# A hybrid decoder layer on one core: low-rank columns as 256 and 448, recurrence and attention values of four heads per 512-column product, the output gate ahead of the queries in every second pair

## The chip, the cores and the metric

The kernel runs on one core of a Trainium2 chip. The metric is the device time in microseconds (us) of one execution; lower is better. The kernel before takes 638.74 us (median of three runs, 638.66 to 638.91).

Engines are named as in the profile: PE is the matrix engine (PEld its loads of the stationary operand), DVE the vector engine, ACT the scalar engine, POOL the GpSimd engine, SP the queue that issues most transfers. "Product" below means one matmul instruction: a stationary block of 128x128 and a moving block of 128 rows and N columns.

## What is computed

One decoder layer on x of 512 tokens by 1024 channels, float32:

```python
h = rms_norm(x, norm_g)
hq, hf, hi, hz, cq, ckv, kr, mz, glog = split(h @ w_in)   # 1024 x4, 384, 256, 64, 1024, 2048 columns
y_a = hgrn2_branch(hq, hf, hi, hz)     # 8 heads of 128: forget gate, query, value, output gate
y_b = mla_branch(cq, ckv, kr, mz)      # 8 heads, causal attention from low-rank columns
gates = sigmoid(glog + b_gate)
merged = gates[0] * (y_a @ w_proj_a) + gates[1] * (y_b @ w_proj_b)
out = rms_norm(x + merged @ w_out, final_norm_g)
```

The HGRN2 branch is a gated linear recurrence in chunks of 32 tokens; the attention branch first widens 384 low-rank query columns and 256 low-rank key/value columns per head (weights `w_uq`, `w_ukv`).

## The kernel before

Every float32 matrix is split in two parts, a rounded high part (`hi`) and the rest (`lo`), and each product of the reference is three products on PE (`mm3`: hi by hi, hi by lo, lo by hi; lines 90 to 92). `load_w` brings 512 KB of weights to `w_raw` (3 buffers) by a transfer on SP, ACT writes `w_hi` (4 buffers, line 111) and DVE `w_lo` (4 buffers, line 112). I call one such load a piece.

There are two kinds of projections of h. `proj_ch` gives channels by tokens: a 128x128 block of weights stands still and 512 tokens of `hT` move, 48 products of 512 columns for 256 channels, from two pieces. `proj_tok` gives tokens by channels: a block of `hT` stands still and the weights move, so the moving block is as wide as the piece of columns, 256 or 192 here. Both write to `mm_ps`, a pool of 3 banks of the accumulator memory; other products write to `ax_ps`, 5 banks.

The stages, in order of the program:

1. Start (lines 195 to 327, engine orders written out by hand): the row `norm_g` is spread over 128 partitions by a product with ones (`ng`, line 274); four token blocks are normalized (`xn`, line 237), transposed (line 245) and split to `hT`; the first 256 low-rank columns are multiplied on the way (line 256). Products of zeros (`idle_mm`, line 221) keep PE running.
2. The other low-rank columns, 256 and then 192 wide, through `proj_tok`.
3. Four pairs of HGRN2 heads (`hg_pair`): forget gates (`proj_ch`), values of two heads (`proj_tok`, 256 columns), queries, output gate, then chunk scores (lines 488 to 496), outputs (507, 509) and the gate's product. `hg_forget` on DVE is long: a scan (432) and a reciprocal (433) among others.
4. Eight attention heads; `mla_values` makes the values of two heads in one call (256 columns), every second head.
5. Two merge projections, the output projection, and the last norm token block by token block.

Outside stage 1 a scheduler that simulates the engines sets the order of instructions on each engine, so the order of the program's text is not the order of the queues.

Of the kernel before, what the change touches and what calls it, by code (L numbers as in the profile page):

```python
# [9 lines left out]
F32 = mybir.dt.float32  # L10
# [8 lines left out]
P = 128  # L19
# [19 lines left out]
def hybrid_layer(ctx: ExitStack, tc: tile.TileContext, a):  # L39
# [92 lines left out]

    def proj_tok(mat, c0, w, lhs, halves=None):

        halves = halves or load_cols(mat, c0, w)
        ps = []
        for t2 in range(NT // 2):
            b = mm_tile()
            for t in range(2):
                tt = 2 * t2 + t  # L140
                for kk in range(KD):
                    mm3(b[:, t * 256 : t * 256 + w], lhs, halves[kk // 4],
                        (slice(None), kk, slice(tt * P, tt * P + P)), (slice(None), kk % 4),
                        kk == 0, kk == KD - 1)
            ps.append(b)
        return ps

# [24 lines left out]
    zero = st.tile([P, 512], BF16, "zero")  # L172
    ones = st.tile([P, P], F32, "ones")
    ones_r = st.tile([P, P], F32R, "ones_r")
    warm = st.tile([P, 1], F32, "warm")
    ng_row = st.tile([1, D], F32, "ng_row")
    ng_z = st.tile([P, D], F32, "ng_z")
    ng_r = [st.tile([P, D], F32R, f"ng_r{i}") for i in range(2)]
    x_sb = [st.tile([P, D], F32, "x", bufs=NT) for _ in range(NT)]
# [15 lines left out]
    load_x(0, 2)  # L195
    nc.scalar.dma_start(ng_row[:], a["norm_g"])
    nc.scalar.dma_start(ident[:], a["c_ident"])
# [53 lines left out]
    def c_product(t, kh, kind, ks=range(4)):  # L251
# [3 lines left out]
        for k in ks:  # L255
            nc.tensor.matmul(ps, hT[l][:, 4 * kh + k, t * P : t * P + P], c_hl[kh][r][:, k * 256 : k * 256 + 256],  # L256
                             start=kh == 0 and kind == 0 and k == 0, stop=kh == 1 and kind == FIN and k == 3)

    FIN = 1
    with tc.manual_schedule(engines={mybir.EngineType.PE, mybir.EngineType.Activation, mybir.EngineType.DVE}):  # L260
        nc.vector.memset(zero[:], 0.0)
        nc.vector.memset(ones[:], 1.0)
        nc.vector.tensor_copy(ones_r[:], ones[:])
        nc.vector.memset(ng_z[:], 0.0)
        for i in range(2):
            nc.vector.tensor_copy(ng_r[i][:], ng_z[:])
        nc.scalar.activation(warm[:], eps, AF.Sqrt)
        idle_mm(6)

        nc.vector.tensor_copy(ng_r[0][0:1], ng_row[:])  # L270
        nc.vector.tensor_tensor(ng_r[1][0:1], ng_row[:], ng_r[0][0:1].bitcast(F32), op=ALU.subtract)
        for x in range(2):
            for n in range(2):
                nc.tensor.matmul(ng[n][:], ones_r[:], ng_r[x][:, half[n]], start=x == 0, stop=x == 1)
            idle_mm(3)

# [35 lines left out]
        for t in range(1, NT):  # L312
            if t + 2 < NT:
                squares(t + 2)
            for kh in range(2):
                lo[kh]()
            if t + 1 < NT:
                scaled(t + 1)
            else:
                c_second = load_cols(w_in, COL_C + 256)  # L320
# [42 lines left out]

    for c0, w in ((0, 256), (256, 256), (512, 192)):
        for t2, ps in enumerate(proj_tok(w_in, COL_C + c0, w, hT, c_second if c0 == 256 else None) if c0 else c_ps):
            nc.scalar.copy(c_sb[:, 2 * t2 : 2 * t2 + 2, c0 : c0 + w],
                           ps[:].rearrange("p (t c) -> p t c", t=2)[:, :, :w])
    css = cw.tile([P, 2, NT], F32, "css")
# [97 lines left out]
    def hg_states(h, k128, ft, v_sb):  # L466
# [7 lines left out]
        for i in range(NT - 1):  # L474
            sl = slice(i * P, i * P + P)
            nc.tensor.matmul(sps[:, sl], kt_[:, sl], v_sb[:, i, (h % 2) * P : (h % 2) * P + P], start=True, stop=True)  # L476
        nc.vector.tensor_copy(st_[:, 0:P], sps[:, 0:P])
# [24 lines left out]
    def hg_out(h, asb, st_, q128, v_sb):  # L502

        ops = ax_tile()
        for i in range(NT):
            sl = slice(i * P, i * P + P)
            nc.tensor.matmul(ops[:, sl], asb[:, sl], v_sb[:, i, (h % 2) * P : (h % 2) * P + P], start=True, stop=i == 0)  # L507
            if i:
                nc.tensor.matmul(ops[:, sl], q128[:, sl], st_[:, i * P - P : i * P], start=False, stop=True)  # L509
# [16 lines left out]
    def silu2(z, pz):  # L526

        nc.scalar.activation(z, pz, AF.Tanh, scale=0.5)
        nc.vector.scalar_tensor_tensor(z, z, 1.0, pz, op0=ALU.add, op1=ALU.mult)

    def hg_pair(pair, before_gate=None, before_out=None):
# [5 lines left out]
        for t2 in range(2):  # L537
            nc.scalar.copy(v_sb[:, 2 * t2 : 2 * t2 + 2].rearrange("p t c -> p (t c)"), vps[t2][:])
# [6 lines left out]
        zz = [z_tile() for _ in hs]  # L545
        for i in range(2):
            silu2(zz[i][:], pz[i][:])
        aa = [hg_scores(h, kk[i][2], kk[i][3], kk[i][4], qq[i][0], qq[i][1]) for i, h in enumerate(hs)]
# [38 lines left out]

    def mla_values(pair):
# [3 lines left out]
        for t2 in range(2):  # L592
            ps = mm_tile()
            for t in range(2):
                tt = 2 * t2 + t
                for k in range(2):
                    mm3(ps[:, t * 256 : t * 256 + 256], cT, wv, (slice(None), 3 + k, slice(tt * P, tt * P + P)),
                        (slice(None), k), k == 0, k == 1)
            split(*[x[:, 2 * t2 : 2 * t2 + 2].rearrange("p t c -> p (t c)") for x in v], ps[:])
        return v  # L600
# [56 lines left out]
    def mla_out(h, pts, v, z):  # L657
        ops = mm_tile()
        for j in range(NT):
            mm3(ops[:, j * P :], v, pts[j], (slice(None), j, slice((h % 2) * P, (h % 2) * P + P)), (slice(None),),  # L660
                j == 0, j == NT - 1)
        nc.vector.tensor_tensor(yb[:, h], ops[:], z[:], op=ALU.mult)
# [28 lines left out]
    for h in range(H):  # L691
# [7 lines left out]
        if h + 1 < H:  # L699
            nope = mla_nope(h + 1, pools[(h + 1) % 2])  # L700
        if h % 2 == 0:
            v = mla_values(h // 2)
        if late:
            mla_out(*late)
        hook = lambda: mla_transpose(pn)
        if h + 1 == H:
# [56 lines left out]

    def out_mm(k, t, n, w):
        mm3(acc[t][n][:], m, w, (slice(None), k, slice(t * P, t * P + P)),
            (slice(None), 0, slice(n * 512, n * 512 + 512)), k == 0, k == KD - 1)

    for k in range(4):
        w = load_wo(k)
        for t in range(NT):  # L770
            for n in range(2):
                out_mm(k, t, n, w)
    ws = [load_wo(k) for k in range(4, KD)]
# [3 lines left out]
    for t in range(NT):  # L777
        ss = op.tile([P, 2], F32, "ss", bufs=2)
        xs = [xr[t][:, n * 512 : n * 512 + 512] for n in range(2)]
        rg = [op.tile([P, 512], F32, f"rg{n}", bufs=2) for n in range(2)]  # L780
        for n in range(2):
            for k in range(4, KD):
                out_mm(k, t, n, ws[k - 4])
            nc.vector.scalar_tensor_tensor(xs[n], acc[t][n][:], 0.5, xs[n], op0=ALU.mult, op1=ALU.add)
            sq = op.tile([P, 512], F32, "sq", bufs=2)
            nc.scalar.activation(sq[:], xs[n], AF.Square, accum_out=ss[:, n : n + 1])
            nc.vector.tensor_tensor(rg[n][:], xs[n], fg[:, n * 512 : n * 512 + 512], op=ALU.mult)
            if n == 0:
                nc.gpsimd.tensor_scalar(ss[:, 0:1], ss[:, 0:1], 1.0 / D, EPS, op0=ALU.mult, op1=ALU.add)
        nc.gpsimd.tensor_scalar(ss[:, 0:1], ss[:, 1:2], 1.0 / D, ss[:, 0:1], op0=ALU.mult, op1=ALU.add)  # L790
        nc.gpsimd.tensor_tensor(ss[:, 0:1], ss[:, 0:1], neg_half[:, 0:1], op=ALU.pow)
        o = a["out"][0, t * P : t * P + P, :]
        nc.scalar.activation(rg[0][:], rg[0][:], AF.Copy, scale=ss[:, 0:1])
        nc.scalar.dma_start(o[:, 0:512], rg[0][:])
        nc.vector.tensor_scalar(rg[1][:], rg[1][:], ss[:, 0:1], None, op0=ALU.mult)
        nc.sync.dma_start(o[:, 512:1024], rg[1][:])
    wop.close()
# [42 lines left out]
```

## Time and profile before

| | |
|---|---|
| median of three runs | 638.74 us |
| profiled execution, its own time | 638.65 us |
| its span, first to last instruction | 636.9 us |
| PE busy | 627.3 us (99%), 3539 products |
| DVE, ACT, POOL busy | 353.9, 239.4, 115.4 us |
| moved by transfers | 59.80 MB, mean 94 GB/s |
| granted PE clock | 0.997 |

The profile is of one execution. A product's duration in it includes its pipeline, and products overlap: what a product costs in a stream is the distance from its start to the next one's start, which is read from the timeline. Busy shares alone say little about a stage; the rows of single instructions are used below.

### The profile page before, as it was taken

To read this page: it belongs to the slowest core of one execution; us is meant where nothing else is said; L and a number is where in the kernel's file an instruction comes from. 1 tells how busy PE (TensorE), PEld (TensorE's weight loads), DVE (VectorE), ACT (ScalarE), POOL (GpSimd) and SP (SyncE) were. 2 spreads that over 40 slices of the span, in tenths; PEclk is the share of its full clock that TensorE was granted. 3 is DMA by queue.
4 is the path that set the end of the run, shared out by engine and by line. 5 is a ranking of instruction groups with operands and counts; after the bars stand their busy time and mean duration, and the time that the engine had idled before them with its cause. 6 is when DMAs were issued, how large, how long until landed. Compare 5 with 4: busy or idle time off the path is not lost.

```text
span 636.9 us, 9069 instructions
## 1 busy us (share of the span) xinstructions
PE 627.3 (99%) x3539; PEld 540.1 (85%) x3539; DVE 353.9 (56%) x550; ACT 239.4 (38%) x453; POOL 115.4 (18%) x213
## 2 busy tenths in 40 slices
PE   8999999999999999999999999999999999999995
PEld 5998988988898898888888988888888888888884
DVE  7716973785486387547485857845322342434244
ACT  5535333232322323345454555534222232323223
POOL 2105310320331132221223132000000010111011
PEclk9999999999999999999999999999999999999998
DMA  7443242233124013312324142133333323324403
GB/s 248 137 125 100 67 138 62 67 99 100 34 68 131 13 55 102 92 45 66 104 56 115 51 138 78 37 100 99 100 98 94 98 75 102 102 95 158 173 11 121
DMA packets 61945, 59.80 MB, mean 94 GB/s; under 512 B 5799, under 2 KB 57293, under 8 KB 61902
## 3 DMA queue, kind: packets, MB, share of 16 engines
q1 hardware_dynamic: 59628, 55.47, 29.3%
q10 hardware_dynamic: 2130, 3.22, 1.6%
q8 instruction: 28, 0.46, 0.3%
q0 software_dynamic: 144, 0.52, 0.3%
q14 instruction: 15, 0.12, 0.1%
HBM read 55.01 MB, written 2.10 MB: 90 GB/s over the span
## 4 chain that ended last, share of the span: by engine, by line
PE 97%; DVE 1%; ACT 0%; issue 0%; POOLq 0%; POOL 0%
PE mm_ps L90 26%; PE mm_ps L92 26%; PE mm_ps L91 26%; PE ax_ps L91 2%; PE ax_ps L90 2%; PE ax_ps L92 2%; PE ax_ps L631 2%; PE mm_ps L256 1%; PE ax_ps L652 1%; PE ax_ps L488 1%; PE ax_ps L507 1%; PE ax_ps L509 1%; PE ax_ps L476 1%; PE ax_ps L496 1%; PE ax_ps L493 1%; PE ax_ps L523 1%
## 5 line engine op out<-in xcount | busy, mean ns | idle before, releaser
L112 DVE TENSOR_TENSOR w_lo<-w_raw,w_hi 128x1024 fp32r<-128x1024 f32 (+3 forms) x92 | 109.0, 1186 | 114.5 <-ACT w_hi L111 110.0
L90 PE MATMUL mm_ps<-hT,w_hi 128*128 128x512 f32 x384 | 151.3, 394 | 0.0
L111 ACT CAST w_hi<-w_raw 128x1024 fp32r<-128x1024 f32 (+3 forms) x92 | 89.8, 977 | 163.0 <-PE mm_ps L91 110.6
L92 PE MATMUL mm_ps<-hT,w_lo 128*128 128x512 f32 x384 | 150.2, 392 | 0.0
L91 PE MATMUL mm_ps<-hT,w_hi 128*128 128x512 f32 x384 | 149.8, 390 | 0.0
L92 PEld LDWEIGHTS mm_ps<-hT,w_lo 128*128 128x128 f32 x384 | 72.1, 188 | 14.8
L91 PEld LDWEIGHTS mm_ps<-hT,w_hi 128*128 128x128 f32 x384 | 72.2, 188 | 14.3
L90 PEld LDWEIGHTS mm_ps<-hT,w_hi 128*128 128x128 f32 x384 | 72.2, 188 | 14.1
L92 PE MATMUL mm_ps<-w_hi,hT 128*128 128x256 f32 (+1 forms) x192 | 54.1, 282 | 0.0
L91 PE MATMUL mm_ps<-w_lo,hT 128*128 128x256 f32 (+1 forms) x192 | 54.0, 282 | 0.0
L90 PE MATMUL mm_ps<-w_hi,hT 128*128 128x256 f32 (+1 forms) x192 | 54.0, 282 | 0.0
L742 POOL TENSOR_TENSOR ma<-ma,z 128x512 f32<-128x512 f32 x8 | 11.8, 1478 | 161.3 <-DVE z L741 161.3
L639 POOL TENSOR_SCALAR p<-p,sm 128x128 f32<-128x128 f32 (+3 forms) x32 | 20.6, 647 | 105.1 <-DVE sm L638 53.5
L91 PEld LDWEIGHTS mm_ps<-w_lo,hT 128*128 128x128 f32 x192 | 36.5, 190 | 0.2
L90 PEld LDWEIGHTS mm_ps<-w_hi,hT 128*128 128x128 f32 x192 | 36.4, 190 | 0.2
L92 PEld LDWEIGHTS mm_ps<-w_hi,hT 128*128 128x128 f32 x192 | 36.5, 190 | 0.0
L433 DVE RECIPROCAL tf<-pr 128x512 f32<-128x512 f32 x8 | 26.8, 3349 | 0.2
L637 ACT ACTIVATE p<-ax_ps,sm 128x128 f32<-128x128 f32 (+3 forms) x32 | 16.8, 528 | 22.0 <-DVE sm L636 21.5
L90 PE MATMUL mm_ps<-ya,w_hi 128*128 128x512 f32 x64 | 25.0, 390 | 0.0
L91 PE MATMUL mm_ps<-ya,w_hi 128*128 128x512 f32 x64 | 24.9, 389 | 0.0
L92 PE MATMUL mm_ps<-ya,w_lo 128*128 128x512 f32 x64 | 24.9, 389 | 0.0
L92 PE MATMUL mm_ps<-yb,w_lo 128*128 128x512 f32 x64 | 24.9, 389 | 0.0
(224 smaller groups left out, 1142.7 us busy)
## 6 DMA issues: line engine op xcount, KB each, us to landing
w_raw<-w_in SPq DMA_DIRECT2D x60, 512.0 KB, 3.8
w_raw<-w_proj_a SPq DMA_DIRECT2D x8, 512.0 KB, 3.5
w_raw<-w_proj_b SPq DMA_DIRECT2D x8, 512.0 KB, 3.4
wo_raw<-w_out SPq DMA_DIRECT2D x8, 512.0 KB, 3.2
w_raw<-w_ukv SPq DMA_DIRECT2D x16, 128.0 KB, 2.5
xr<-x SPq DMA_DIRECT2D x4, 512.0 KB, 6.5
x<-x SPq DMA_DIRECT2D x3, 512.0 KB, 8.7
w_raw<-w_uq SPq DMA_DIRECT2D x8, 192.0 KB, 2.6
```

Of the source, the lines that this page charges most:

```text
L90: nc.tensor.matmul(ps, lh[lsl], rh[rsl], start=start, stop=False)
L91: nc.tensor.matmul(ps, lh[lsl], rl[rsl], start=False, stop=False)
L92: nc.tensor.matmul(ps, ll[lsl], rh[rsl], start=False, stop=stop)
L111: nc.scalar.copy(hi[:, :o], raw[:, :o])
L112: (lo_eng or nc.vector).tensor_tensor(lo[:, :o], raw[:, :o], hi[:, :o].bitcast(F32), op=ALU.subtract)
L256: nc.tensor.matmul(ps, hT[l][:, 4 * kh + k, t * P : t * P + P], c_hl[kh][r][:, k * 256 : k * 256 + 256], start=kh == 0 and kind == 0 and k ...
L433: nc.vector.reciprocal(rp[:], pr[:])
L476: nc.tensor.matmul(sps[:, sl], kt_[:, sl], v_sb[:, i, (h % 2) * P : (h % 2) * P + P], start=True, stop=True)
L631: nc.tensor.matmul(sps[:, :n], qh[:, bl], kpe[x][:, :n], start=False, stop=x == 1)
L637: nc.scalar.activation(p[:, :n], sps[:, :n], AF.Exp, scale=SCALE, bias=sm[:, 1:2], accum_out=sm[:, 2:3])
L639: nc.gpsimd.tensor_scalar(p[:, :n], p[:, :n], sm[:, 3:4], 0.5, op0=ALU.mult, op1=ALU.mult)
L742: nc.gpsimd.tensor_tensor(ma[:, j], ma[:, j], g[:], op=ALU.add)
```

## The change

What moves, in the order of the program:

- The start spreads `norm_g` by products over 64 instead of 128 rows: its two halves stand in rows 0 and 32, and `pick` chooses one. The preparation on DVE works on 64x512 instead of 128x1024; zeros and ones come from POOL. One idle product instead of three stands between the two pairs of products, four instead of three after them.
- The remaining 448 low-rank columns are one product per token block and k, from four pieces of 2 k by 448 columns instead of four pieces of 4 k by 256 or 192.
- `proj_tok` takes 512 columns, values of four heads, two token blocks at a time, from four pieces of 2 k by 512. It is called in pairs 0 and 2 only, and its result stays for the next pair.
- In pairs 1 and 3 the output gate's projection stands in the place of the values, between forget gates and queries.
- `mla_values` makes values of four heads in one call, at heads 0 and 4, with one buffer instead of two, and is called behind the output product of the head before.
- In the last norm both halves of a token block share a buffer, and for the last block ACT scales 384 columns and DVE 640 instead of 512 each.

```diff
-    def proj_tok(mat, c0, w, lhs, halves=None):
-        halves = halves or load_cols(mat, c0, w)
-        ps = []
+    def proj_tok(mat, c0, lhs, done):
+        v = mat[:, c0 : c0 + 512].rearrange("(k p) c -> p k c", p=P)
+        w = []
         for t2 in range(NT // 2):
...
+            ps = [mm_tile() for _ in range(2)]
+            for k in range(KD):
+                if t2 == 0 and k % 2 == 0:
+                    w.append(load_w(v[:, k : k + 2, :]))
+                for t in range(2):
+                    tt = 2 * t2 + t
+                    mm3(ps[t][:], lhs, w[k // 2], (slice(None), k, slice(tt * P, tt * P + P)), (slice(None), k % 2),
+                        k == 0, k == KD - 1)
             for t in range(2):
...
+                done(2 * t2 + t, ps[t])
...
+        for i in range(2):
+            nc.vector.tensor_copy(ng_r[i][:], zf[:])
...
         for x in range(2):
             for n in range(2):
-                nc.tensor.matmul(ng[n][:], ones_r[:], ng_r[x][:, half[n]], start=x == 0, stop=x == 1)
-            idle_mm(3)
+                nc.tensor.matmul(ng[n][:], pick_r[:, n], ng_r[x][:], start=x == 0, stop=x == 1)
+            idle_mm(1 + 3 * x)
...
-    for c0, w in ((0, 256), (256, 256), (512, 192)):
...
+    c_second += [load_c2(j) for j in range(2, 4)]
+    for t in range(NT):
+        ps = mm_tile()
+        for k in range(KD):
+            mm3(ps[:, 0:448], hT, c_second[k // 2], (slice(None), k, slice(t * P, t * P + P)), (slice(None), k % 2),
+                k == 0, k == KD - 1)
+        nc.scalar.copy(c_sb[:, t, 256:704], ps[:, 0:448])
...
-        vps = proj_tok(w_in, COL_I + cc, 256, hT)
-        v_sb = hw.tile([P, NT, 256], F32, "v", 2)
...
+        if pair % 2 == 0:
+            for t in range(NT):
+                v_sb[t] = hw.tile([P, 512], F32, f"v{t}")
+            proj_tok(w_in, COL_I + cc, hT, lambda t, ps: nc.scalar.copy(v_sb[t][:], ps[:]))
+        else:
+            zz = gate()
         pq = proj_ch(w_in, COL_Q + cc, hT)
...
-        pz = proj_ch(w_in, COL_ZA + cc, hT)
...
+        if pair % 2 == 0:
+            zz = gate()
...
-        wv = load_w(w_ukv[:, :, 2 * pair : 2 * pair + 2, 128:256])
-        v = [mw.tile([P, NT, 256], F32R, f"v{i}", 2) for i in range(2)]
+        wv = load_w(w_ukv[:, :, h0 : h0 + 4, 128:256])
+        v = [mw.tile([P, NT, 512], F32R, f"v{i}") for i in range(2)]
...
+        c = 384 if last else 512
+        nc.scalar.activation(rg[:, :c], rg[:, :c], AF.Copy, scale=ss[:, 0:1])
+        nc.scalar.dma_start(o[:, :c], rg[:, :c])
+        nc.vector.tensor_scalar(rg[:, c:], rg[:, c:], ss[:, 0:1], None, op0=ALU.mult)
+        nc.sync.dma_start(o[:, c:], rg[:, c:])
```

How the queues change shows at three places. The first is PE at the start of the low-rank columns (stage 2). In a row, `mm_ps` with its number is the accumulator tile of a token block, `w_hi` and `w_lo` with their numbers are a piece, and a number at the end is the moving width. Before:

```order
L334 MATMUL ax_ps_398<-ident_103,rows_98 128x38
L90 MATMUL mm_ps_426<-w_hi_359,hT0_119 128x256
L91 MATMUL mm_ps_426<-w_lo_360,hT0_119 128x256
L92 MATMUL mm_ps_426<-w_hi_359,hT1_120 128x256
L90 MATMUL mm_ps_426<-w_hi_359,hT0_119 128x256
```

Now:

```order
L347 MATMUL ax_ps_401<-ident_103,rows_98 128x38
L90 MATMUL mm_ps_441<-w_hi_362,hT0_123 128x448
L91 MATMUL mm_ps_441<-w_lo_363,hT0_123 128x448
L92 MATMUL mm_ps_441<-w_hi_362,hT1_124 128x448
L90 MATMUL mm_ps_441<-w_hi_362,hT0_123 128x448
L91 MATMUL mm_ps_441<-w_lo_363,hT0_123 128x448
L92 MATMUL mm_ps_441<-w_hi_362,hT1_124 128x448
L90 MATMUL mm_ps_441<-w_hi_368,hT0_123 128x448
L90 MATMUL mm_ps_467<-w_hi_362,hT0_123 128x448
L91 MATMUL mm_ps_467<-w_lo_363,hT0_123 128x448
```

A piece now holds two k instead of four; the scheduler turns to the second token block (467) before the first is done, and the last piece (436, 437) is first read after 42 products.

The second place is PE at the scores of pair 1 (`qi`, `ki`, `ko` and the 64-wide `q64`, `k64` are operands of the scores; `v` and `kt` belong to the states). Before:

```order
L476 MATMUL ax_ps_1568<-v_1465,kt_1563 128x128 x3
L488 MATMUL ax_ps_1644<-qi_1533,ki_1318 128x128 x4
```

Now:

```order
L92 MATMUL mm_ps_1548<-hT0_123,w_lo_1557 128x512
L494 MATMUL ax_ps_1449<-v0_763,kt_1444 128x128
L494 MATMUL ax_ps_1449<-v1_764,kt_1444 128x128
L494 MATMUL ax_ps_1449<-v2_765,kt_1444 128x128
L506 MATMUL ax_ps_1457<-qi_1414,ki_1244 128x128 x4
L511 MATMUL ax_ps_1457<-qi_1414,ko_1245 32x32 x8
L514 MATMUL ax_ps_1457<-q64_1416,k64_1247 64x64 x4
L506 MATMUL ax_ps_1475<-qi_1423,ki_1273 128x128 x4
L511 MATMUL ax_ps_1475<-qi_1423,ko_1274 32x32 x8
L514 MATMUL ax_ps_1475<-q64_1425,k64_1276 64x64 x4
L90 MATMUL mm_ps_1671<-w_hi_1674,hT0_123 128x512
```

Before, the 48 products ahead of these states and scores were those of the output gate. Now (tile 1548, piece 1557) they are the forget products of pair 2, which the scheduler has moved ahead of the scores of pair 1; the values of pair 2 (tile 1671) follow the scores.

The third place is DVE around the same scores; `asb` is the masked score block that the outputs need, `f`, `pr`, `tf`, `ki` belong to the forget gates of the next pair. Before:

```order
L480 SCALAR_TENSOR_TENSOR st_1569<-st_1569,ft_1345,ax_ps_1568 128x128
L529 SCALAR_TENSOR_TENSOR z_1639<-z_1639,mm_ps_1577 128x512
L497 COPY_PREDICATED asb0_730<-mask_le_405,ax_ps_1644 128x512
L480 SCALAR_TENSOR_TENSOR st_1569<-st_1569,ft_1345,ax_ps_1568 128x128
L497 COPY_PREDICATED asb1_734<-mask_le_405,ax_ps_1662 128x512
```

Now:

```order
L446 TENSOR_SCALAR f_1610<-tf_1609,c1_421,c2_423 128x512
L450 SCALAR_TENSOR_TENSOR pr_1616<-f_1610,fr_633 128x512
L451 RECIPROCAL tf_1617<-pr_1616 128x512
L495 COPY st_1450<-ax_ps_1449 128x128
L112 TENSOR_TENSOR w_lo_1729<-w_raw_1727,w_hi_1728 128x1024
L515 COPY_PREDICATED asb0_637<-mask_le_408,ax_ps_1457 128x512
L466 TENSOR_TENSOR ki_1630<-k_1611,tf_1617 128x512
L498 SCALAR_TENSOR_TENSOR st_1450<-st_1450,ft_1271,ax_ps_1449 128x128
L515 COPY_PREDICATED asb1_641<-mask_le_408,ax_ps_1475 128x512
```

A scan, a reciprocal and the last piece of the values now stand ahead of `asb0` on DVE.

More of the change, by code (lines that the diff above doesn't have):

```diff
@@ L319, in hybrid_layer @@
             else:
-                c_second = load_cols(w_in, COL_C + 256)
+                c_second = [load_c2(j) for j in range(2)]
             for kind in (0, 1, 2):
@@ L534, in hg_pair, with gate @@
         kk = [hg_forget(h, pf[i]) for i, h in enumerate(hs)]
[L535 to L538 removed]
+        def gate():
+            pz = proj_ch(w_in, COL_ZA + cc, hT)
+            zz = [z_tile() for _ in hs]
+            for i in range(2):
+                silu2(zz[i][:], pz[i][:])
+            return zz
+        if pair % 2 == 0:
[4 more added lines that the diff above has]
+            zz = gate()
         pq = proj_ch(w_in, COL_Q + cc, hT)
```

108 lines of the change are left out of this document (48 added, 60 removed).

## Prediction

> **What bounds the kernel now.** I read the shares first, then the chain that ended last, then what PE waited for.
>
> ```profile
> PE 627.3 (99%) x3539; PEld 540.1 (85%) x3539; DVE 353.9 (56%) x550; ACT 239.4 (38%) x453; POOL 115.4 (18%) x213
> PE 97%; DVE 1%; ACT 0%; issue 0%; POOLq 0%; POOL 0%
> PE ax_ps L221 <- DVE zero L261: 1.2, 1, 1.2
> PE ax_ps L274 <- DVE ng_r L270: 0.7, 1, 0.7
> PE ax_ps L245 <- DVE xn L237: 0.4, 1, 0.4
> ...
> ```
>
> The second row is the chain's share by engine, the others are PE's waits (total, times, longest). The longest three are 2.3 us together and all belong to the start, as do the two left out. Behind the start PE runs one stream of products without a break that the profile names, so a saving must come from what a product costs in this stream, from the start, or from the 7 us behind the last product. A product costs the distance between starts. The timeline of PE gives it for each width:
>
> ```profile
> 27.30 0.39 PE L90 MATMUL mm_ps<-w_hi,hT 128*128 128x256 f32 x1
> 38.91 0.25 PE L90 MATMUL mm_ps<-w_hi,hT 128*128 128x192 f32 x1
> 49.61 0.41 PE L90 MATMUL mm_ps<-hT,w_hi 128*128 128x512 f32 x1
> 50.78 0.40 PE L92 MATMUL mm_ps<-hT,w_lo 128*128 128x512 f32 x1
> ...
> 117.97 0.28 PE L90 MATMUL mm_ps<-w_hi,hT 128*128 128x256 f32 x1
> 129.48 0.40 PE L90 MATMUL mm_ps<-hT,w_hi 128*128 128x512 f32 x1
> ...
> 290.09 0.36 PE L90 MATMUL mm_ps<-w_hi,cT 128*128 128x256 f32 x1
> 291.61 0.40 PE L90 MATMUL ax_ps<-kn,qn 128*128 128x128 f32 x2
> ...
> 308.95 0.33 PE L90 MATMUL mm_ps<-pt,v 128*128 128x384 f32 x1
> 309.48 0.28 PE L90 MATMUL mm_ps<-pt,v 128*128 128x256 f32 x1
> ...
> 616.23 0.39 PE L90 MATMUL ax_ps<-wo,m 128*128 128x512 f32 x1
> 629.61 0.39 PE L92 MATMUL ax_ps<-wo,m 128*128 128x512 f32 x1
> ```
>
> Width 256: 96 products from 27.30 to 38.91, 0.121 us each, and 96 from 117.97 to 129.48, 0.120. Width 192: 96 from 38.91 to 49.61, 0.1115. Width 384: three from 308.95 to 309.48, 0.177. Width 512: 616.23 and 629.61 are the first and the last of 60 products, 13.38/59 = 0.2268; right behind the low-rank columns, 49.61 to 50.78, five take 0.234 each. So two products of 256 cost 0.240 and one of 512 costs 0.227 to 0.234: 6 to 13 ns less per pair, and 192 costs almost as much as 256.
>
> **Low-rank columns.** Removed: 22.31 us (27.30 to 49.61). Added: 4 token blocks x 8 k x 3 = 96 products of 448 columns, a width the trace lacks. Between its neighbours 384 and 512: (0.177 + 0.227)/2 = 0.202; on the line from 256 to 512: 0.120 + 0.75 x 0.107 = 0.200. At 0.201 they take 19.3 us. Gain 3.0; ends 2.8 (0.203) and 3.2 (0.199). The copies of the result to `c_sb` and the four pieces are as many elements as before, on ACT and DVE. The last piece must wait for a slot in the 3 raw buffers, as the last one did before, but its first use stands 42 products (8.4 us) into the stage, against a cast and a subtraction of 2.3 us (rows below).
>
> **Values of the recurrence.** Removed: 4 x 11.51 = 46.04 us. Added: 2 x 96 products of 512. At 0.2268 they take 43.55, at 0.234 they take 44.9; gain between 1.1 and 2.5. Most products of that stage follow each other in a stream, so I take 0.2285, near the lower price: 43.9, gain 2.2.
>
> **Values of attention.** Removed: 12 products from 290.09 to 291.61, 1.52 us, and 84 more at 0.120: 11.6. Added: 48 of 512, 10.9 to 11.2. Gain 0.7 (0.4 to 0.7), and I keep 0.6.
>
> **The start.** Here the row of `norm_g` is late:
>
> ```profile
> 2.63 1.29 DVE L266 CAST ng_r<-ng_z 128x1024 fp32r<-128x1024 f32 x2
> 3.84 0.68 DVE L270 CAST ng_r<-ng_row 1x1024 fp32r<-1x1024 f32 x1
> 4.55 1.21 DVE L271 TENSOR_TENSOR ng_r<-ng_row,ng_r 1x1024 fp32r<-1x1024 f32 x1
> 5.47 0.19 ACT L280 ACTIVATION_READ_ACCUMULATOR sq<-x 128x1 f32 x1
> 5.69 0.13 DVE L281 TENSOR_SCALAR rsq<-rs 128x1 f32<-128x1 f32 x1
> 6.54 1.41 PE L274 MATMUL ax_ps<-ng_r,ones_r 128*128 128x512 f32 x2
> 7.56 1.41 DVE L237 SCALAR_TENSOR_TENSOR xn<-x,rs,ax_ps 128x512 f32<-128x512 f32 x2 [0.59 <-PE ax_ps L274]
> 10.61 0.36 SPq L208 DMA_DIRECT2D maskf<-c_masks  x1
> SPq L208 <- DMA w_raw<-w_in: 1.1, 1, 1.1
> 11.32 1.14 ACT L224 CAST w_hi<-w_raw 128x512 fp32r<-128x512 f32 x2
> ```
>
> `xn` waited 0.59 us for the spread row. Half the width makes DVE's two casts of 0.65 each half as long, so the real row's conversion starts near 3.0 instead of 3.84 (POOL's fill of zeros and ones must land first) and ends about 0.8 us earlier; the statistics chain behind it, which began at 5.69 only because DVE was busy, then begins with the second sum (5.66). Both together allow `xn` near 6.8: 0.75 us earlier. One idle product between the pairs instead of three lets the second pair follow. A bound from above is the transfer of the second piece, landed at 10.6 (SP's wait), for ACT's cast at 11.32: 0.7. From below: nothing gained, if POOL's fill or the row's transfer comes late. I take 0.6. Later stages follow it one to one, since their waits are on the same chain.
>
> **Behind the last product.**
>
> ```profile
> 632.58 0.72 ACT L793 ACTIVATE rg<-rg,ss 128x512 f32<-128x512 f32 x1 [1.10 <-POOL ss L791]
> 632.58 0.49 DVE L795 TENSOR_SCALAR rg<-rg,ss 128x512 f32<-128x512 f32 x1 [1.13 <-POOL ss L791]
> 633.09 0.33 SPq L796 DMA_DIRECT2D out<-rg  x1
> 633.33 0.34 ACTq L794 DMA_DIRECT2D out<-rg  x1
> ```
>
> ACT's transfer leaves last. With 384 columns ACT needs about 0.58, DVE with 640 about 0.6, so both leave near 633.2: gain 0.1 (0 to 0.2).
>
> **What is moved, and its cover.** These groups (count, busy, mean ns) price the work beside PE, and two rows of PE's timeline begin and end the scores of a pair:
>
> ```profile
> L112 DVE TENSOR_TENSOR w_lo<-w_raw,w_hi 128x1024 fp32r<-128x1024 f32 x74 | 93.3, 1263 | 106.4 <-ACT w_hi L111 106.2
> L433 DVE RECIPROCAL tf<-pr 128x512 f32<-128x512 f32 x8 | 26.8, 3349 | 0.2
> L432 DVE TENSOR_TENSOR_SCAN pr<-f,fr 128x512 f32<-128x512 f32 x8 | 9.8, 1222 | 5.7 <-POOL fr L429 5.7
> L497 DVE COPY_PREDICATED asb<-mask_le,ax_ps 128x512 f32<-128x512 uint8 x8 | 5.8, 731 | 5.1 <-PE ax_ps L496 5.1
> L111 ACT CAST w_hi<-w_raw 128x1024 fp32r<-128x1024 f32 x74 | 77.8, 1052 | 148.9 <-PE mm_ps L91 100.0 <-issue 34.6 <-PE mm_ps L92 13.8
> L538 ACT COPY v<-mm_ps 128x512 f32<-128x512 f32 x8 | 4.7, 584 | 2.1 <-PE mm_ps L92 2.1
> ...
> 153.38 1.06 PE L488 MATMUL ax_ps<-qi,ki 128*128 128x128 f32 x8
> 157.72 0.50 PE L90 MATMUL mm_ps<-hT,w_hi 128*128 128x512 f32 x1
> ```
>
> The values of four heads read a new piece every 12 products, 2.7 us, in their first half, and hold all four slots. The last piece waits for the forget product's last slot, then 1.05 us on ACT and 1.26 on DVE, possibly behind a reciprocal of 3.35: 5.7 us, needed after 36 products, 8.2 us. Covered, with 2.5 us to spare. In the second half the fourth token block needs the bank of the first, whose copy takes 0.58, one group of three products (0.68) plus 0.68 after it ended: 0.8 us to spare. Pieces of the following product get a slot 2.7 us into the second half and need 2.3 of the 8.2 left.
>
> In pair 1 the gate no longer stands between queries and scores; the queue of PE shows pair 2's 48 forget products there, 10.9 us, and the query chain is an ACT instruction and a few of DVE and POOL of the sizes above. But on DVE the forget chain of pair 2 now stands ahead of `asb0`. It starts when the first forget tile is done, 12 products (2.7 us) before the last; then f (taken as long as `asb0`), scan, reciprocal, `w_lo` and `asb0` take 0.73 + 1.22 + 3.35 + 1.26 + 0.73 = 7.3; with ACT's part and hand-overs I call it 8.6. PE asks for it after those 2.7 us, the scores (157.72 - 153.38 = 4.3) and 25 products (5.7): 12.7. Covered, 4.1 us to spare. On SP the gate's pieces of the odd pairs pass those of the queries; both go to the same raw buffers, which DVE's subtraction frees, so SP is paced as before, and the values of attention need half as many transfers of twice the size.
>
> Covers seldom hold everywhere: I add 0.3 us for waits at new places, between 0 and 1.
>
> **Sum.** 3.0 + 2.2 + 0.6 + 0.6 + 0.1 - 0.3 = 6.2 us against the profiled execution's 638.65 (its span of 636.9 and 1.75 around it): 632.45; that run is 0.09 below the median, so I say 632.5. Extremes of the terms give 7.35 (3.2 + 2.5 + 0.7 + 0.75 + 0.2) and 3.3 (2.8 + 1.1 + 0.4 - 1): 631.4 to 635.4.
>
> **Rivals.** (a) A product costs its columns and nothing else. The columns are as many as before (96 x 448 = 96 x 256 + 96 x 192, 384 x 256 = 192 x 512), so the 5.8 us vanish and the start and end alone leave 0.4 to 0.8: 638. Against it: 0.1115 for 192, 0.120 for 256 and 0.227 for 512 do not lie on a line through zero. The Trainium skill, "TensorE: Matmul & The Clock Gate", section "Back-to-back issue gap", is near this rival: warm, the gap is columns over 2.4 per ns plus 2.5 ns, which would price 192, 256, 448 and 512 at 82, 109, 189 and 216 ns; an estimate by it leaves 0.9 us of the 5.8. The rows disagree with it in this kernel (0.1115 against 82 ns). Chance 0.03.
>
> (b) The value products wait for pieces or banks. If the second reciprocal slips ahead of a piece, each call loses 3.35 less the 2.5 to spare up to the whole 3.35; two calls, 2 to 6 us: 634.2 to 638. For it: four pieces in 8.2 us where two were needed in 11.5. Against it: DVE is 56% busy. Chance 0.11.
>
> (c) Slower than before: on DVE, `asb0` and the states come so late behind pair 2's forget chain that PE stands at the outputs of pair 1. A whole chain of the second head as well (f, scan, reciprocal and three more like `asb0`: 7.5 us) and the two query pieces behind it (1.05 + 1.26 each: 4.6) would be 12.1 against 4.1 to spare: 8 us lost, 640.5. It decides from 7.5 us lost. Against it: the queue puts the second head's chain behind both `asb`. Chance 0.03.
>
> **How the numbers follow.** Forecast, 631 to 634: 0.78; better still, below 631, if the start gains 0.9 and transitions between pieces fall away: 0.05; (b) 0.11, of which half lies below 635.4; (a) and (c) 0.03 each. The range 630.9 to 635.4 holds about 0.84. This kernel's times can be told apart from about 0.2%, 1.3 us: faster than 637.4 in 0.94, the same in 0.03, slower in 0.03.
>
> **What would show it.** Right: 96 products of 448 about 0.201 apart; value products at 0.227 to 0.23; 48 products fewer on PE; the first `xn` near 6.9; PE without new waits behind the start. Wrong: PE waiting on `w_lo` or `w_hi` in the value products (b), on `asb` in the outputs of pair 1 (c), or 448 columns 0.215 or more apart (a).

## The result, and the profile after

| | median us | lowest to highest | ratio to before, 95% interval |
|---|---|---|---|
| before | 638.70 | 638.65 to 639.28 | |
| changed | 643.71 | 642.48 to 646.70 | 1.0083 (1.0059 to 1.0107) |

The change made the kernel 0.8% slower. The profiled run of it took 644.26 us, its span was 642.5. Busy time and the chain's shares on the page of the changed kernel:

```profile
PE 627.0 (98%) x3202; PEld 527.0 (82%) x3202; DVE 352.8 (55%) x548; ACT 239.1 (37%) x451; POOL 119.3 (19%) x217
...
PE 96%; ACT 1%; DVE 1%; POOL 1%; issue 0%; DMA 0%; POOLq 0%; DVEq 0%; ACTq 0%
```

PE's longest waits in it (us in total, times, longest):

```profile
PE ax_ps L541 <- DVE k L533: 3.4, 2, 2.0
PE ax_ps L676 <- POOL p L663: 2.7, 1, 2.7
PE ax_ps L227 <- DVE zero L273: 1.2, 1, 1.2
PE mm_ps L90 <- ACT pt L151: 0.4, 1, 0.4
```

Before, PE had no wait behind the start that the list names. Now three rows are new: the transposes of the last pair's normalised outputs (`k`, L541) wait for DVE, the last transposes of the last attention head's `p` (L676) for POOL, and the first product that reads them for ACT. They make 6.5 us, but the kernel lost 5 us and should have gained 6, so I compared the traces at equal work. Behind the start both kernels stream 1,298,470 columns through PE; this is how much later (+) or earlier (-) the changed kernel started the same column, by the starts of the products:

| time in the kernel before, us | 20 | 70 | 290 | 300 | 420 | 430 to 620 |
|---|---|---|---|---|---|---|
| changed | +0.9 | -2.1 | -5.8 | +0.5 | +0.3 | +5.6 |

The low-rank columns gave 3.0 us, and by 290 us the kernel was 5.8 ahead although its start was 0.9 late. All of that and more was lost in two places of a few microseconds each. (Where the order of unlike products differs the lead moves by 1 or 2 us without any wait; single steps are read with that in mind.)

The first place is the end of pair 3. PE's rows there, in the changed kernel (start, duration, operation, idle time before it):

```profile
284.84 0.39 PE L527 MATMUL ax_ps<-st,q 128*128 128x128 f32 x2
287.18 0.66 PE L541 MATMUL ax_ps<-ident,k 128*128 128x128 f32 x4 [1.95 <-DVE k L533]
289.27 1.11 PE L541 MATMUL ax_ps<-ident,k 128*128 128x128 f32 x4 [1.44 <-DVE k L533]
```

and in the kernel before:

```profile
280.66 0.39 PE L509 MATMUL ax_ps<-st,q 128*128 128x128 f32 x2
...
287.03 0.60 PE L523 MATMUL ax_ps<-ident,k 128*128 128x128 f32 x4
```

Before, 27 products stood between the last output and the first transpose: 17 of a gate, 10 that widen low-rank columns. The gate is not this pair's but that of the first attention head, as the time shows at which ACT first reads each finished gate. Before (two of the pair, then the attention head's):

```profile
267.09 0.59 ACT L528 ACTIVATE z<-mm_ps 128x512 f32<-128x512 f32 x1
268.92 0.59 ACT L528 ACTIVATE z<-mm_ps 128x512 f32<-128x512 f32 x1
285.68 0.59 ACT L528 ACTIVATE z<-mm_ps 128x512 f32<-128x512 f32 x1
```

and now (the second of the pair, then the attention head's):

```profile
246.27 0.59 ACT L546 ACTIVATE z<-mm_ps 128x512 f32<-128x512 f32 x1
276.79 0.59 ACT L546 ACTIVATE z<-mm_ps 128x512 f32<-128x512 f32 x1
```

The pair's gate left its place, the attention head's gate and the widening products moved up into it, and nothing is left behind the outputs. What the transposes need (four sums of squares on ACT, the power on POOL, the product on DVE) takes 4.4 us from the last outputs of the second head, 4.2 before. For the first head it takes 6.4 instead of 4.1, since ACT now works on the attention head's exponentials between its squares. That alone would not lengthen the stall, which ends with the second head.

The second place is the last attention head. PE in the changed kernel, and behind it DVE and POOL:

```profile
420.83 0.49 PE L676 MATMUL ax_ps<-ident,p 128*128 128x128 f32 x3
423.97 0.66 PE L676 MATMUL ax_ps<-ident,p 128*128 128x128 f32 x4 [2.65 <-POOL p L663]
425.03 0.68 PE L90 MATMUL mm_ps<-pt,v 128*128 128x512 f32 x1 [0.40 <-ACT pt L151]
425.51 0.63 PE L90 MATMUL mm_ps<-ya,w_hi 128*128 128x512 f32 x1
425.94 0.63 PE L91 MATMUL mm_ps<-ya,w_hi 128*128 128x512 f32 x1
...
428.77 0.40 PE L92 MATMUL mm_ps<-ya,w_lo 128*128 128x512 f32 x1
```

```profile
417.71 3.38 DVE L152 TENSOR_TENSOR ya<-ya,ya 128x512 fp32r<-128x512 f32 x5
421.02 0.15 DVE L662 RECIPROCAL sm<-sm 128x1 f32<-128x1 f32 x1
421.09 2.34 DVE L112 TENSOR_TENSOR w_lo<-w_raw,w_hi 128x1024 fp32r<-128x1024 f32 x2
421.34 2.58 POOL L663 TENSOR_SCALAR p<-p,sm 128x512 f32<-128x512 f32 x1 [1.98 <-PE ax_ps L676]
```

The same two steps in the kernel before:

```profile
414.81 0.15 DVE L638 RECIPROCAL sm<-sm 128x1 f32<-128x1 f32 x1
415.15 0.69 POOL L639 TENSOR_SCALAR p<-p,sm 128x512 f32<-128x512 f32 x1 [4.95 <-DVE sm L638]
```

The reciprocal stood behind five splits of `ya` before as well. But then 49 products of `hT` lay between the head's last scores and its last transposes; now 21 do. They are of the 72 that make the last gates: without the value products of head 6, 51 of them have been used up ahead of the scores, where it was 20. A second thing happened at the same time: POOL's step took 2.58 us beside DVE's two subtractions and 0.69 before, when DVE stood still, so 1.9 of the 2.65 us are POOL's own. An estimate from these rows is a wait of about 0.75 us without that. No run separates the two, as e2 and e9, which bring the cover back, also take this step away from the subtractions.

Both waits have an aftermath. Windows of the changed kernel (stretch, its length, busy us and count of PE, PEld, DVE, ACT and POOL, then the granted clock, the DMA share and GB/s):

```profile
286.00:288.60 2.60, 0.66 (x4) 0.42 (x4) 1.42 (x3) 1.79 (x7) 1.60 (x3) 1.00 0.33 76
288.60:292.00 3.40, 2.73 (x13) 2.73 (x14) 2.19 (x5) 1.17 (x2) 0.00 (x0) 0.51 0.00 0
...
425.40:428.60 3.20, 3.20 (x9) 2.43 (x9) 1.23 (x3) 0.34 (x1) 0.00 (x0) 0.50 0.49 153
428.60:431.00 2.40, 2.40 (x12) 1.97 (x11) 0.00 (x0) 0.00 (x0) 0.00 (x0) 1.00 0.00 0
```

After each wait PE runs at half clock for more than 3 us in this profile: at the last head its rows above start 0.43 us apart where 0.227 is usual. The Trainium skill ("TensorE: Matmul & The Clock Gate", "Part 1: The HAM clock gate") describes such a gate: half rate after an idle window of about 3.4 us, by a window that runs freely. The stretches' length agrees; that a whole window must be idle does not, since the longest single wait was 2.65 us (and 2.44 us, straight behind products of 512 columns, was enough in e1). With a free window it would be chance whether half clock follows a wait. The runs, which now differ by 4 us, fit that: the fastest, 642.48, has a mean clock of 0.995, the slowest, 646.70, one of 0.986.

### The profile page after: what moved, and what is told of

Same layout as the page of the kernel before. It is cut to its first block, busy times and chain, and to the rows that moved or that the text cites. A ratio compares the mean times of both kernels' runs of the same rounds, so it can differ in the third digit from the quotient of the medians.

```text
span 642.5 us, 8392 instructions
## 1 busy us (share of the span) xinstructions
PE 627.0 (98%) x3202; PEld 527.0 (82%) x3202; DVE 352.8 (55%) x548; ACT 239.1 (37%) x451; POOL 119.3 (19%) x217
## 4 chain that ended last, share of the span: by engine, by line
PE 96%; ACT 1%; DVE 1%; POOL 1%; issue 0%; DMA 0%; POOLq 0%; DVEq 0%; ACTq 0%
PE mm_ps L90 26%; PE mm_ps L92 25%; PE mm_ps L91 25%; PE ax_ps L90 2%; PE ax_ps L92 2%; PE ax_ps L91 2%; PE mm_ps L262 2%; PE ax_ps L655 2%; PE ax_ps L676 1%; PE ax_ps L506 1%; PE ax_ps L525 1%; PE ax_ps L494 1%; PE ax_ps L514 1%; PE ax_ps L527 1%; PE ax_ps L541 1%; PE ax_ps L251 1%
## 5 line engine op out<-in xcount | busy, mean ns | idle before, releaser
L91 PE MATMUL mm_ps<-w_lo,hT 128*128 128x512 f32 (+1 forms) x96 | 36.5, 382 | 0.0
L92 PE MATMUL mm_ps<-w_hi,hT 128*128 128x512 f32 (+1 forms) x96 | 36.4, 382 | 0.0
L90 PE MATMUL mm_ps<-w_hi,hT 128*128 128x512 f32 (+1 forms) x96 | 36.4, 386 | 0.0
L90 PE MATMUL mm_ps<-ya,w_hi 128*128 128x512 f32 x64 | 25.7, 401 | 0.0
L91 PE MATMUL mm_ps<-ya,w_hi 128*128 128x512 f32 x64 | 25.5, 399 | 0.0
L90 PE MATMUL mm_ps<-yb,w_hi 128*128 128x512 f32 x64 | 24.9, 389 | 0.0
L91 PE MATMUL mm_ps<-yb,w_hi 128*128 128x512 f32 x64 | 24.9, 389 | 0.0
L152 DVE TENSOR_TENSOR wo<-wo_raw,wo 128x1024 fp32r<-128x1024 f32 x8 | 9.6, 1224 | 25.9 <-ACT wo L151 25.9
```

Of the source, the lines that this page charges most:

```text
L90: nc.tensor.matmul(ps, lh[lsl], rh[rsl], start=start, stop=False)
L91: nc.tensor.matmul(ps, lh[lsl], rl[rsl], start=False, stop=False)
L92: nc.tensor.matmul(ps, ll[lsl], rh[rsl], start=False, stop=stop)
L152: nc.vector.tensor_tensor(lo, src, hi.bitcast(F32), op=ALU.subtract)
```

## Experiments

All are edits of the changed kernel, named e1 to e12; each ran beside the kernel before on the same chip (medians of that between 638.67 and 638.86), and the ratios are to it.

**e1: gate of pair 3 put back behind the states.**

```diff
-        else:
+        if not (pair % 2 == 0 or pair == 3):
             zz = gate()
...
-        if pair % 2 == 0:
+        if pair % 2 == 0 or pair == 3:
             zz = gate()
```

> The output gate of pair 3 stands behind the states again, as in the kernel before; pair 1 keeps it ahead of the queries. Theory (cover): the stall behind pair 3 (waits of 2.1 and 1.6 us, then about 3.4 us at half the product rate, so 1.7 lost) came because the gate's products were no longer there to hide the normalisation of the outputs. 27 products stand between outputs and transposes again, about 6 us, so 5.4 us come back. The stall at the last head gets 9 more products (2 us) against its wait of 2.8, so it may shrink too, by up to 2 us and its slow stretch. Time 634.5 to 638.5, likeliest 637. Rival (the values of four heads cost the time: their pieces or banks make PE wait): nothing changes, 643.7. Rival (the normalisation itself became late on DVE and POOL): the same waits stand in front of the transposes, 642 or more.

Measured: 639.64 (637.72 to 640.55), ratio 1.0009 (0.9997 to 1.0021). The waits at L541 are gone, 4.1 us came back, 2.6 fewer than the likeliest value of the expectation. PE's waits in this kernel show why:

```profile
PE mm_ps L90 <- DVE f L477: 3.2, 2, 2.4
PE mm_ps L90 <- ACT pt L151: 1.2, 1, 1.2
```

The last head keeps a wait, for ACT. And there are two new ones in pair 3, 3.2 us together; e3 shows them alone.

**e2: values of attention for two heads again.**

```diff
... (`mla_values` makes the values of two heads, as in the kernel before)
-        if late:
-            mla_out(*late)
-        if h % 4 == 0:
-            v = mla_values(h)
+        if h % 2 == 0:
+            v = mla_values(h // 2)     # 24 products of 256, as before
+        if late:
+            mla_out(*late)
```

> The values of attention are made for two heads at a time again (24 products of 256 at heads 0, 2, 4, 6) and everything else stays as in the changed kernel. Theory (cover): at head 6 these 24 products (2.9 us) stood beside the softmax; moved to head 4 they were missing there, the last head's scores came later in the queue and their softmax was no longer hidden. With them back the waits of 2.8 and 0.56 us at the last head and the slow stretch behind them (1.6) go: 5.0 us less, 0.6 more for the narrow products: 639.3 (638.5 to 640.5), with the stall behind pair 3 still there. Rival (the wait comes from the splits of `ya` that stand on DVE ahead of the reciprocal, which the kernel before had too): the wait at the last head stays above 2 us and the time is 643.7 to 644.5.

Measured: 638.07 (637.57 to 639.40), ratio 0.9989 (0.9979 to 0.9998): 5.6 us below the changed kernel and 0.4 below the expected range. The queue of PE at the last head is that of the kernel before again and the only wait left behind the start is that at L541. The splits of `ya` were not the cause by themselves: they stand where they stood.

**e3: both edits.**

> Both edits together: the gate of pair 3 behind the states, and the values of attention for two heads at a time. Theory (cover): both stalls gone, PE without a wait over 0.3 us behind the start: 643.7 - 5.4 - 5.0 + 0.6 = 633.9 (633 to 635), and runs agree within 0.5 us since no slow stretch is left. Rival (covers are only passed on: a wait taken away here comes back at the next place): over 637.

Measured: 638.16 (636.45 to 639.38), ratio 0.9989 (0.9978 to 1.0000). The rival was right: both old waits are gone, and the cover is missing elsewhere. PE in this kernel:

```profile
247.99 0.50 PE L90 MATMUL mm_ps<-cT,w_hi 128*128 128x512 f32 x1 [0.71 <-DVE f L477]
254.16 0.50 PE L90 MATMUL mm_ps<-hT,w_hi 128*128 128x512 f32 x1 [2.46 <-DVE f L477]
```

Each product needs a bank that still holds a query's product, and DVE's reading of it (L477) stands in its queue behind the chain of the forget gates. In the kernel before, the 11.5 us of this pair's value products ran ahead of the queries. The pair lost them to pair 2, so it lacks cover twice: ahead of its queries and behind its outputs. One gate cannot stand in both places.

**e4: e3, and the spread of `norm_g` on 128 rows** (`pick`, `pick_r`, `ng_r` and `zf` with 128 partitions instead of 64).

> As the one before, and the rows that spread `norm_g` fill 128 partitions (zeros below) instead of 64, same widths and same number of instructions. Theory (the clock): the four spreading products on 64 rows did not count as enough work, so PE went to full rate at 12.1 us instead of 8.4, which cost the eight transposes and the first products about 0.9 us. With 128 rows full rate comes near 8 us, the transposes are 0.11 apart instead of 0.21, and the time is 0.9 to 1.5 us below that of the one before: 632.6 (632.0 to 633.1). Rival (the start is late because of the fills on POOL or the single idle product between the pairs): no change against the one before, 633.9, and full rate still comes at 12 us.

Measured: 638.36 (637.18 to 639.40), ratio 0.9994 (0.9985 to 1.0004), no change against 638.16. The start's 0.9 us is not explained by the 64 rows. The same start showed both faces. Its first transposes in the changed kernel, then in e3, then those of the old start in the kernel before:

```profile
8.74 1.91 PE L251 MATMUL ax_ps<-ident,xn 128*128 128x128 f32 x8
```

```profile
8.00 1.06 PE L251 MATMUL ax_ps<-ident,xn 128*128 128x128 f32 x8 [0.88 <-DMA ident<-c_ident]
```

```profile
8.67 1.04 PE L245 MATMUL ax_ps<-ident,xn 128*128 128x128 f32 x8
```

By the distances of its products PE came to full rate at 4.3 to 4.9 us in five profiles with the new start and at 9.5 to 12.0 in six; with the old one at 8.2 and 8.6, and in e4 at 6.0. When it comes early, the identity's transfer is the next limit. Why the new start falls into two groups stays open.

**e5: the gate of pair 3 in two halves,** with the values of attention for two heads as in e2.

```diff
+        def gate1(h):     # as mla_gate: 128 columns, 24 products, one z
...
-        else:
-            zz = gate()
+        elif pair == 1:
+            zz = gate()
+        else:
+            zz = [gate1(hs[0])]
         pq = proj_ch(w_in, COL_Q + cc, hT)
...
+        elif pair == 3:
+            zz.append(gate1(hs[1]))
```

> In pair 3 the output gate is computed for each head by itself, 24 products each: head 6's ahead of the queries, head 7's behind the states. The values of attention go by two heads, all else as in the changed kernel. Theory (pair 3 has lost the 11.5 us of value products between its forget gates and its queries and needs cover in two places: about 3.5 us ahead of the queries, as the waits of 0.88 and 2.6 with the whole gate behind the states show, and about 4.0 us behind the outputs, as the waits of 2.1 and 1.6 with the whole gate ahead show): 24 products of 0.227 (5.4 us) cover the first, and 12 of 0.227 with 12 of 0.12 (4.2 us) now stand behind the outputs. No wait over 0.4 us behind the start, no slow stretch: 633.0 to 634.5, median 633.7, and runs within 1.4 us of each other (the start). Rival (half a gate is too little at one of the places): a wait of 1 to 2.5 us at one of them, with a slow stretch in some runs: 635 to 637.5.

Measured: 634.24 (633.75 to 634.72), ratio 0.9933 (0.9920 to 0.9945). The list of PE's waits names none behind the start that is longer than 0.2 us. PE in this kernel:

```profile
280.11 0.39 PE L527 MATMUL ax_ps<-st,q 128*128 128x128 f32 x2
284.54 1.04 PE L541 MATMUL ax_ps<-ident,k 128*128 128x128 f32 x8
```

Products fill the 4.3 us between them: 12 that widen low-rank columns and 12 of the attention values. They are not the gate's; its second half stands ahead of the outputs and holds them back. This kernel beats both others: 4.5 us below the kernel before, 9.5 below the changed one.

**e6, e7, e10 and e8: the parts of the sum, each against e5.** First, e5 with the start of the kernel before:

> As e5, with the start of the kernel before (row of `norm_g` spread from one row over 1,024 columns). Theory: the new start brings 0.6 us at most, so 0.3 to 0.8 above e5, 634.2; and it varies by 1.3 us from run to run, as the kernel before does, since PE's rise to full rate falls anywhere from 4 to 12 us in the profiles taken so far. Rival (the new start costs, as the 0.9 us in the first profile of the changed kernel seem to say): 0.5 or more below e5.

Measured: 634.10 (633.48 to 634.61), ratio 0.9929 (0.9916 to 0.9943). The new start brings nothing that can be told (-0.1 us).

e5 with the low-rank columns as 256, 256 and 192:

> As e5, with the low-rank columns in three pieces of 256, 256 and 192 again. Theory (a narrow product costs more than its columns): 3.0 us more than e5 (2.7 to 3.3), 636.7. Rival (a product costs its columns alone): the same as e5.

Measured: 636.72 (636.39 to 637.21), ratio 0.9968 (0.9958 to 0.9979): the wider products are worth 2.5 us.

e5 with the values of the recurrence by two heads and the gate behind the states everywhere:

> As e5, with the values of the recurrence by two heads in every pair and the gate behind the states in every pair, as in the kernel before; the low-rank columns and the start are those of the changed kernel. Theory (product widths): 384 products of 256 (46.0 us) stand for 192 of 512, which took 44.1 in the profile of the changed kernel: 1.9 us above e5, 636.1 (635.6 to 636.7). Rival (a product costs its columns alone): the same as e5.

Measured: 635.80 (635.51 to 636.30), ratio 0.9955 (0.9941 to 0.9968): worth 1.6 us.

e5 with the values of attention for four heads:

> As e5, with the values of attention for four heads again. Theory: only the stall at the last head is there, a wait of 1.4 to 2.8 us for the normalised scores, 0.6 behind it, and 1.7 lost to the slow stretch in most runs, less 0.6 for the wide products: 3.5 to 5 us above e5, 637.2 to 638.7. Rival (the stall at the last head came from the delay behind pair 3, not from the values): 0.6 below e5, 633.1.

Measured: 638.97 (636.93 to 639.66), ratio 1.0001 (0.9992 to 1.0010): it costs 4.7 us. PE in this kernel:

```profile
416.63 0.55 PE L689 MATMUL ax_ps<-ident,p 128*128 128x128 f32 x3 [1.43 <-POOL p L676]
418.26 0.66 PE L689 MATMUL ax_ps<-ident,p 128*128 128x128 f32 x4 [1.09 <-POOL p L676]
419.32 0.50 PE L90 MATMUL mm_ps<-pt,v 128*128 128x512 f32 x1 [0.40 <-ACT pt L151]
```

The stall at the last head is there with nothing late in pair 3, so it belongs to this edit. POOL's two last normalisations, 0.59 and 0.69 us in the kernel before, take 6.0 together here, beside DVE's splits and subtractions:

```profile
412.18 6.03 POOL L676 TENSOR_SCALAR p<-p,sm 128x384 f32<-128x384 f32 x2 [7.65 <-DVE sm L675]
```

The profiled run is the fastest, 636.93, without a slow stretch; the seven runs with a mean clock of 0.991 to 0.995 took 638.7 to 639.7, the other three 636.9 to 638.1.

**e9: values of attention by four, two and two heads.**

```diff
... (`mla_values` takes the number of heads and the tile)
+        if h == 6:
+            v = mla_values(6, 2, v)      # second half of the same tile
         if late:
             mla_out(*late)
         if h % 4 == 0:
-            v = mla_values(h)
+            v = mla_values(h, 2 if h else 4)
```

> As e5, and the values of attention go by four heads for heads 0 to 3 (48/2 = 24 products of 512), but by two for heads 4 and 5 and for heads 6 and 7 (24 products of 256 each), these last at head 6. Theory (the stall at the last head comes because 24 products are missing at head 6): 49 products stand behind the last head's scores and ahead of its last transposes again, where e8 has 21 (and e5 51), so no wait there; the wide products of heads 0 to 3 bring 0.4 us against e5: 633.8 (633.2 to 634.4). Rival (the tile for four heads or its wide products themselves delay the last head): the wait of 1.4 to 2.8 us is still there, 636.5 to 639.

Measured: 635.75 (635.15 to 636.65), ratio 0.9956 (0.9943 to 0.9968). With 24 products at head 6 again the wait for `p` is gone, as the theory says. But the kernel is 1.5 us slower than e5. One row of PE:

```profile
417.89 0.50 PE L90 MATMUL mm_ps<-pt,v 128*128 128x512 f32 x1 [1.57 <-ACT pt L151]
```

Here no product stands between the last transposes and the product that reads them; in e5 three do. The 0.4 us of the wide products cannot be seen. (This profile gives a granted clock of 0.946, but its 96 products of 448 columns take the 19.36 us of the other profiles, so nothing is read from that figure.)

**e11 and e12: products without a purpose in the waits.** Behind pair 3, on e2:

```diff
         yps = ax_tile()
+        for _ in range({6: 8, 7: 7}.get(h, 0)):
+            nc.tensor.matmul(yps[:], hT[0][:, 0, 0:P], hT[0][:, 0], start=True, stop=True)
```

> As e2 (gate of pair 3 ahead of the queries, attention values by two heads), with 15 products of 512 columns whose result is overwritten, ahead of the transposes behind pair 3, where e2 waits 2.0 and 1.6 us (15 x 0.227 = 3.4). The work needed is as late as in e2. Theory (an idle PE is put at half rate for a stretch of 3.4 us or more afterwards): the waiting time itself stays lost but PE keeps full rate, so 1.7 us less than e2: 636.4 (635.9 to 637.0). Rival (the slow products behind the wait have another cause, such as transposes or contention for memory): as e2, 638.1, or later by what the fill delays.

Measured: 638.42 (637.54 to 638.87), ratio 0.9989 (0.9980 to 0.9999): as e2. The clock stayed at 1.00 there, but behind the fill PE waited anyway:

```profile
285.03 3.69 PE L541 MATMUL ax_ps<-hT 128*128 128x512 f32 x15
...
291.31 0.38 PE L90 MATMUL ax_ps<-kn,qn 128*128 128x256 f32 x1 [0.48 <-DVE ya L544]
291.91 0.39 PE L90 MATMUL mm_ps<-w_hi,cT 128*128 128x256 f32 x1 [0.22 <-DVE qn L152]
```

By these two profiles the half clock costs 0.6 us behind pair 3 (from the row of the last outputs to the same product of the next scores it is 9.1 us in e2, 284.11 to 293.24, and 8.6 in e11, 284.88 to 293.44), not the 1.7 that half of 3.4 us suggests: the short products there wait for DVE in any case. The run times show no gain at all.

The same at the last head, on e8:

```diff
+        if fill:      # last head only, ahead of the transposes
+            for _ in range(14):
+                nc.tensor.matmul(tps[2][:], hT[0][:, 0, 0:P], hT[0][:, 0], start=True, stop=True)
```

> As e8, with 14 products of 512 columns, whose result is overwritten, in front of the last head's transposes (14 x 0.227 = 3.2 us, where the profile of e8 waits 1.4, 1.1 and 0.4); the later transposes have fewer products between them. Theory (after a wait PE is at half rate for a stretch in most runs of e8, where products of 512 of the first projection, which wait for nothing else, take 0.427 instead of 0.227): the waiting time stays lost, the stretch goes, and the runs lie together near the fastest of e8 (636.9): 637.2 median (636.5 to 637.8), spread below 1.4 us. Rival (as e11 showed behind pair 3, the work behind the wait is held back by DVE and ACT anyway): as e8, 638.5 to 639.5.

Measured: 639.06 (638.29 to 639.71), ratio 1.0004 (0.9995 to 1.0013). In part as expected: no run has a mean clock below 0.996 (0.991 to 0.998 without the fill), and the spread fell from 2.7 to 1.4 us. But the median did not fall, since the fill moved real products and the wait for ACT became 1.6 us:

```profile
412.98 3.34 PE L688 MATMUL ax_ps<-hT 128*128 128x512 f32 x14
...
422.00 0.50 PE L90 MATMUL mm_ps<-pt,v 128*128 128x512 f32 x1 [1.57 <-ACT pt L151]
```

What the slow stretch alone costs at the last head, 1.6 us by eight products at 0.427 instead of 0.227 in the changed kernel, was not isolated in the run times; the two groups of e8's runs lie 1.2 us apart by their medians.

## Why the prediction was wrong

It said 632.5 and gave slower 0.03. By its own steps:

- **Low-rank columns, 3.0.** Right in kind. First and last of the 96 products of 448 in the changed kernel:

```profile
28.22 0.47 PE L90 MATMUL mm_ps<-w_hi,hT 128*128 128x448 f32 x1
...
47.58 0.36 PE L92 MATMUL mm_ps<-w_hi,hT 128*128 128x448 f32 x1
```

  19.36/95 = 0.204 us each against the 0.201 taken, so 19.6 us and 2.75 gained; 2.5 in run times.
- **Values of the recurrence, 2.2.** The 192 products took 0.230 each, 44.1 us: 1.9 gained by the rows, 1.6 in run times; within the ends of 1.1 and 2.5.
- **Values of attention, 0.6.** The 48 products took 0.231 each, 11.1 us, so 0.5 against the 11.6. But the edit is worth -4.7 in run times: its cover was never looked at.
- **Start, 0.6.** `xn` began at 7.15 instead of 7.56, not at 6.8 (6.81 to 7.13 in the other profiles of this start). What followed was set by the time of PE's rise to full rate, which the sum left out. Nothing gained (e6).
- **Tail, 0.1.** From the start of the last product to the end it is 7.26 us in both. Nothing.
- **Waits at new places, -0.3 (0 to -1). This step failed.** e5, without the two stalls, is 9.5 us below the changed kernel: 4.7 behind pair 3 (643.71 of the changed kernel less 638.97 of e8) and 4.7 at the last head (638.97 less 634.24 of e5, what the wide products gain there already off). I priced the cover of the moved gate at pair 1, where the next pair's forget products came in its place, and found 4.1 us to spare; that held, pair 1 has no wait. Pair 3 has no next pair. And the values of attention I priced as products only, though 24 of them leave head 6. How much of the second 4.7 is the missing cover and how much POOL's slower step beside DVE stays open.

Of the rivals, (a) is refuted: three widths and two experiments (2.5 and 1.6 us) show that columns alone are not the price, and the gap by the formula of the Trainium skill ("TensorE: Matmul & The Clock Gate", "Back-to-back issue gap"), 189 ns for 448 columns, does not hold for these products (204). The page gives that formula for a single product in isolation, which the prediction did not say; and 2.5 ns for each of 336 products is 0.84 us, not 0.9. (b) did not occur: no wait for a piece or a bank in the value products. (c) foresaw a stall for want of cover and a slower kernel, but at pair 1 and by late scores on DVE; that its price of 8 us is near the 9.5 is luck, as half of the 9.5 lies at the last attention head. That PE has 48 products fewer was a slip: it is 337 (96, 192 and 48, and one idle).

The terms that held, with the start and the tail at nothing and the values of attention undone, give 638.7 - 2.5 - 1.6 = 634.6; e5 took 634.24. The parts add up to within 0.4 us.

## What to carry to other kernels

A block of products that goes away or moves is also the cover of every chain that ran beside it: for each place that it leaves, the last repetition of the loop included, list what runs on the other engines there and what PE would do instead. What stands in a place need not be the block that was moved: other products move up into the gap and are then missing where they stood. One block can't cover two places, but its halves can, and that was worth 3.9 us here (e5 against e3), about as much as the wider products. Compare two traces at equal work done, not at equal time: it shows in one table which stage gained and where the gain was lost.

## What the runs showed of the hardware

- PE falls to half clock for about 3.4 us after a wait of 2.44 to 2.65 us (e1, the changed kernel), or two of 1.8 to 1.95 and 1.44 close together (e2, the changed kernel), in some runs of the same kernel and not in others. The profile of e3 has a wait of 2.46 and no such stretch; by the mean clock, e3 took 636.5 to 638.0 in five runs (mean clock 0.998) and 638.3 to 639.4 in the other five (0.994 or 0.995). What it costs depends on whether PE bounds the work in the stretch: 0.6 us behind pair 3, by one profile of each kind.
- The rise to full rate at the start falls anywhere from 4.3 to 12 us by run, worth up to 1.6 us at the same code (the first product of 448 columns starts at 26.60 in e3 and at 28.22 in the changed kernel).
- POOL's normalisation of 512 columns took 0.68 to 0.70 us in the fifteen other rows of the two traces and 2.58 where DVE ran two subtractions of 1,024 columns beside it. The Trainium skill ("GPSIMD Engine Reference", "8. Key points") says that POOL shares its ways into SBUF with DVE and that it contends with DVE instructions of two SBUF inputs, which these subtractions are; these rows agree.
